# Seven-product up-projection in pairs of chunks: chunks 4 to 19 as eight interleaved pairs, 256-column weight blocks, low parts added by DMA

## The chip, the core and the metric

The kernel runs on one core of a Trainium2 chip. The metric is the device time of one execution in microseconds; the kernel before took 1119.47 us (median of three runs, 1118.79 to 1120.16). Engines are named as in the profile: PE is TensorE (matmuls), DVE is VectorE, ACT is ScalarE, POOL is GpSimd, SP is SyncE. SP issues the plain loads; POOL issues the DMAs that add to their target and some stores.

## The reference

Two decoder layers over a residual stream of 512 tokens by 1024 features: layer 0 with dilated window attention, layer 1 with forgetting attention, each followed by the same feed-forward block. Only that block concerns us here:

```python
def conv_ffn(xn, w_up, cw, cb, w_down):          # xn (1, 512, 1024), w_up (1024, 2 * 2816)
    a = xn @ w_up
    ap = jnp.pad(a, ((0, 0), (CONV_W - 1, 0), (0, 0)))
    a = sum(ap[:, j:j + T] * cw[j] for j in range(CONV_W)) + cb
    gate, val = jnp.split(a, 2, axis=-1)
    return (jax.nn.gelu(gate, approximate=True) * val) @ w_down
```

All data are 32-bit floats. The block's output goes through a root-mean-square norm with a gain (`norm_gains[l, 3]`) and is added to the residual.

## The kernel before

**Precision.** TensorE takes 32-bit operands in a reduced format. Each operand is therefore split into a high part (a copy to that format, made by ScalarE) and a low part (the operand less its high part). A product is three matmuls per 128 rows of the contraction: high by high, high by low, low by high (`mm3`, lines 283 to 285). A weight's low part is made in one of two ways: VectorE subtracts (`sub_low`, `Weights.low`), or ScalarE writes the negative of the raw weight, scaled copy with -1, in the reduced format, and a DMA issued by GpSimd adds the raw weight onto it (`add_low` at line 680, `Weights.low_added` at line 98).

**Chunks.** The up-projection runs over 22 chunks (`NF`). Chunk c has 128 gate columns and the 128 value columns with the same index, so two PSUM banks of 128 by 512 (features by tokens). After a chunk's products come its taps: ScalarE's Identity with the last tap and the bias (line 620), two VectorE operations that add the other two taps (621, 623), for the gate half and for the value half; then ScalarE's Gelu of the gate half (641) and VectorE's product of the halves (638), stored to `hD` in DRAM by a GpSimd DMA (636).

**Two ways to multiply.** A plain chunk (`up`) takes two weights of eight 128-row blocks, 48 matmuls over 512 tokens. A chunk of the tuple `SEVEN` is a 2 by 2 block product (gate and value by the two halves of the contraction; the two halves of the tokens) done with seven products in place of eight: 84 matmuls over 256 tokens. It needs sums of weight blocks, S1 to S4, on VectorE; sums of the activations, XA and XB, made once per layer (`sums_in`); and additions between partial results, done by VectorE in PSUM (lines 963 to 1007). Before, eleven chunks of each layer go by seven products, mostly two of them followed by a plain one; `weights_a` and `weights_b` prepare a chunk's weights one or two chunks ahead, and the generator `steps` places their parts between the products.

**Order and buffers.** All is under a manual schedule: each engine executes its instructions in the order of the program text, and waits where an operand is not ready. Pools give out buffers in the same order. `t8` (pool p8) has sixteen buffers of 8 KB per partition, for split weights and activations; in the up-projection eight of these hold the activations and their sums. `t4` (pool p4) has ten of 4 KB: raw weights, sums of weights (`wsum`), the taps' result `bb`, gains, and others outside this stage. `t2` has eight of 2 KB. PSUM has eight banks. A buffer can be given to a new tile after its tile's last use in program order; the new tile's first writer then waits until that use has really ended, a DMA's reading included.

**Weights.** `Weights` walks the list `pieces` in order. `load(n)` has SyncE issue loads up to piece n, `take(k)` hands out the next k raw pieces after loading `ahead_dma` further ones, `high_added()` splits a piece in the way with the DMA, and `get()` returns the next split piece.

**The end of the stage.** While the last chunks run, `pair_load`, `pair_sums`, `pair_highs` and `pair_lows` prepare the first steps of the down-projection (`down`), whose results go to the norm object `nxt`; its gain was loaded before `ffn` began.

Of the kernel before, what the change touches and what calls it, by code (L numbers as in the profile page):

```python
# [16 lines left out]
T = 512  # L17
# [10 lines left out]
SEVEN = 4, 5, 7, 8, 10, 11, 13, 14, 16, 17, 19  # L28

ADDED = (6, 9, 12, 15, 18), (18, 20)  # L30
# [87 lines left out]
def trunk_kernel(ctx, tc, x, norm_gains, w_qkv_a, w_o_a, w_q_b, w_o_b, kv_norm, w_kvf, b_f,  # L118
# [35 lines left out]
    def add(f):  # L154
        pieces.append(f)
# [22 lines left out]

    dT = [tc.dram_tile([ND, 128, 2048], F32, name=f"dT{l}") for l in range(2)]

    def add_ffn(l):
        for c in range(NF):
            add_cols(w_up[l], c * 128)
            add_cols(w_up[l], DFF + c * 128)

        for j in range(ND):
            add(lambda raw, j=j: [(raw[:, 0:512], w_down[l][j * 256:j * 256 + 128, 0:512]),
                                  (raw[:, 512:1024], dT[l][j, :, 0:512])])
            add(lambda raw, j=j: [(raw, dT[l][j, :, 512:1536])])
        add_rows(w_down[l], range(1, NF, 2))  # L190
# [420 lines left out]
    def ffn(l, bd, cp, nxt, ahead):  # L611
# [4 lines left out]
        def taps(c, banks, between=None):  # L616
            bb = t4([128, 2, T], name="bb")
            for s, ch in ((0, c), (1, NF + c)):
                ps = banks[s]
                act.activation(bb[:, s, :], ps, AF.Identity, bias=cp[:, 3, ch:ch + 1], scale=cp[:, 2, ch:ch + 1])  # L620
                dve.scalar_tensor_tensor(bb[:, s, 1:], ps[:, :T - 1], cp[:, 1, ch:ch + 1], bb[:, s, 1:],  # L621
                                         ALU.mult, ALU.add)
                dve.scalar_tensor_tensor(bb[:, s, 2:], ps[:, :T - 2], cp[:, 0, ch:ch + 1], bb[:, s, 2:],  # L623
                                         ALU.mult, ALU.add)
                if s == 0 and between is not None:
                    between()
            return bb

        gated = []

        def product():

            if gated:
                c, bb = gated.pop()
                if c - 1 in hc:
                    pool.dma_start(hD[c - 1], hc.pop(c - 1))
                hc[c] = t2([128, T], name="hc")
                dve.tensor_tensor(hc[c], bb[:, 0, :], bb[:, 1, :], ALU.mult)

        def glu(c, bb):  # L640
            act.activation(bb[:, 0, :], bb[:, 0, :], AF.Gelu_apprx_tanh)
            gated.append((c, bb))

        def post(c, banks, between=None):
            product()
            glu(c, taps(c, banks, between))
# [23 lines left out]
        halves, rest, late = {}, {}, []  # L670

        def split_pair(pair, src, n=1024):
            act.copy(pair[:, 0, :n], src)
            yield
            dve.tensor_tensor(pair[:, 1, :n], src, pair[:, 0, :n].bitcast(F32), ALU.subtract)

        def add_low(w, raw):

            act.activation(w[:, 1], raw, AF.Copy, scale=-1.0)
            pool.dma_start(w[:, 1], raw, accum_op=ALU.add)  # L680

        def sub_low(w, raw, n=1024):
            dve.tensor_tensor(w[:, 1, :n], raw, w[:, 0, :n].bitcast(F32), ALU.subtract)

        def weights_a(c):


            if c >= NF:
                return
            if c not in SEVEN:  # L690
                for i in range(2):
                    if c in ADDED[i]:
                        W.high_added()
                    else:
                        W.high()
                        W.low()
                    yield
                return
            r0, r1 = W.take(2)
            w = [t8([128, 2, 1024], F32R, name="w") for _ in range(2)]  # L700
            sa, sb = (t4([128, 1024], name="wsum") for _ in range(2))
            a11, a12, a21, a22 = r0[:, 0:512], r0[:, 512:1024], r1[:, 0:512], r1[:, 512:1024]
            act.copy(w[0][:, 0], r0)
            if c - 1 not in SEVEN:
                add_low(w[0], r0)
            dve.tensor_tensor(sa[:, 0:512], a11, a21, ALU.subtract)
            dve.tensor_tensor(sb[:, 0:512], a21, a22, ALU.add)
            yield
            dve.tensor_tensor(sa[:, 512:1024], sb[:, 0:512], a11, ALU.subtract)
            if c - 1 not in SEVEN:  # L710
                act.copy(w[1][:, 0], sa)
                add_low(w[1], sa)
            v = [t.rearrange("p s (q k c) -> p s q k c", q=2, k=4) for t in w]
            halves[c] = dict(A11=v[0][:, :, 0], A12=v[0][:, :, 1], S3=v[1][:, :, 0], S2=v[1][:, :, 1])
            rest[c] = w, r0, a12, a22, sa, sb

        def weights_b(c):

            if c not in rest:
                return  # L720
            (w0, w1), r0, a12, a22, sa, sb = rest.pop(c)
            if c - 1 in SEVEN:
                act.copy(w1[:, 0], sa)
                sub_low(w0, r0)
            w = [t8([128, 2, 1024], F32R, name="w") for _ in range(2)]
            dve.tensor_tensor(sb[:, 512:1024], a12, sa[:, 512:1024], ALU.subtract)
            act.copy(w[1][:, 0, 0:512], a22)
            if c - 1 in SEVEN:
                sub_low(w1, sa)
            yield  # L730
            act.copy(w[0][:, 0], sb)
            if c - 1 in SEVEN:
                late.append(lambda: sub_low(w[0], sb))
            else:
                add_low(w[0], sb)
            sub_low(w[1], a22, 512)
            v = [t.rearrange("p s (q k c) -> p s q k c", q=2, k=4) for t in w]
            halves[c].update(S1=v[0][:, :, 0], S4=v[0][:, :, 1], A22=v[1][:, :, 0])
            yield

# [186 lines left out]
        post(0, first[0:2])  # L930
        next(extra)
        post(1, first[2:4])
        W.ahead = 1
        W.split(base + 7)
        W.high_added()
        steps = iter(())
        begun = None
        before = None
        for c in range(2, NF):
            if c == NF - 4:  # L940
                pair_load(0)
            steps = chain(steps, weights_b(c + 1), weights_a(c + 2))
            if c + 2 == SEVEN[0]:
                steps = chain(steps, weights_b(c + 2))
            if c in SEVEN:
                w = halves.pop(c)
                W.n_get += 2
                x11, x21, x22 = [(xT[0][i], xT[1][i], s) for i, s in ((0, LO), (1, LO), (1, HI))]
                if begun:
                    banks, s1, s17 = begun  # L950
                else:
                    banks = [bank([128, T], name="up") for _ in range(2)]
                    s1, s17 = (t2([128, 256], name="csum") for _ in range(2))
                s12 = t2([128, 256], name="csum")
                o1, o2, o3, o4 = banks[0][:, LO], banks[0][:, HI], banks[1][:, LO], banks[1][:, HI]

                def prod(o, a, x, start=False, w=w):
                    half_mm(o, w[a], x[0:2], x[2], start)

                def begin():  # L960
                    act.copy(s1, o1)
                    prod(o3, "S3", (*XA, HI), True)
                    dve.tensor_tensor(s17, o3, s1, ALU.add)
                    prod(o2, "S2", (*XB, HI))

                def join():
                    dve.tensor_tensor(s12, o2, s1, ALU.add)

                if begun:
                    prod(o2, "S2", (*XB, HI))  # L970
                    product()
                    join()
                    bb = taps(*before)
                else:
                    prod(o1, "A11", x11, True)
                    product()
                    bb = taps(*before, begin)
                    join()
                prod(o3, "A22", (*XB, LO))
                prod(o1, "A12", x21)  # L980
                prod(o2, "S1", (*XA, LO))
                next(steps, None)
                glu(before[0], bb)
                next(steps, None)
                if c + 1 in SEVEN:
                    next(steps, None)
                dve.tensor_tensor(o4, o2, s17, ALU.add)
                if c + 1 in SEVEN:
# [10 lines left out]
                if c + 1 not in SEVEN:  # L999
                    next(steps, None)  # L1000
# [7 lines left out]
            else:  # L1008
                banks = [bank([128, T], name="up") for _ in range(1 if begun else 2)]
                if begun:  # L1010
                    w, first = begun
                    banks = [first, *banks]
# [802 lines left out]
```

## Time and profile before

| What | Value |
|---|---|
| median of three runs | 1119.47 us (1118.79 to 1120.16) |
| span of the profiled execution, first to last instruction | 1116.5 us |
| TensorE busy | 1100.3 us, 99% of the span |
| VectorE busy | 894.2 us, 80% |
| ScalarE busy | 680.4 us, 61% |
| GpSimd busy | 214.7 us, 19% |
| granted TensorE clock, mean | 0.998 |
| chain that ended last | PE 85%, DMA 6%, DVE 4%, issue 3% |

The profiled execution is shown by its span alone; its own whole time is not listed beside the runs, and the median of the runs lies 3.0 us above the span. A row of a timeline gives the start and the duration in us, the engine, the line of the kernel, the operation, output and inputs by the program's names, and in brackets the idle time before it and what ended it. Durations on one engine overlap, since an instruction's beginning runs beside the end of the one before: what an instruction costs its engine is the distance from start to start. The up-projection of layer 0 lies at about 208 to 417 us of the span, that of layer 1 at about 794 to 1005.

### The profile page before, as it was taken

The numbers are of one execution on the slowest core, as the hardware profiler recorded it, in microseconds if no ns is written. First come the engines' busy times: TensorE is split into PE (matmuls) and PEld (weight loads), VectorE is DVE, ScalarE is ACT, GpSimd is POOL, SyncE is SP. The second block draws the span as 40 slices with busy tenths as digits, with TensorE's granted clock in tenths as the row PEclk, the third lists the DMA queues.
The fourth block names the chain that finished last, engine by engine and source line by source line (L and its number), as shares of the span: only waits on it lengthen the run. The fifth ranks groups of instructions, "written<-read, shape, count | busy, mean of one in ns | idle before, by whom it ended". The sixth has DMA issues, their size and how long they took to land.

```text
span 1116.5 us, 18086 instructions
## 1 busy us (share of the span) xinstructions
PE 1100.3 (99%) x6545; PEld 958.5 (86%) x6545; DVE 894.2 (80%) x1509; ACT 680.4 (61%) x1128; POOL 214.7 (19%) x315
## 2 busy tenths in 40 slices
PE   9899999999999999999999999999999999999997
PEld 6788889999999988888878888889999999978886
DVE  5797778887788679997698687868887788679894
ACT  6454466656666747576462588756656666747572
POOL 2723000411111211000000545500411111211000
PEclk9999999999999999999999999999999999999999
DMA  5699964368878979894447666594468878979862
GB/s 193 234 371 408 348 190 122 82 179 204 199 186 188 249 254 320 297 321 113 132 151 256 216 161 168 186 283 120 84 180 203 202 183 188 244 242 321 314 245 75
DMA packets 186209, 240.46 MB, mean 215 GB/s; under 512 B 12608, under 2 KB 132408, under 8 KB 186120
## 3 DMA queue, kind: packets, MB, share of 16 engines
q1 hardware_dynamic: 171016, 186.61, 51.4%
q0 software_dynamic: 15104, 52.70, 20.7%
q8 instruction: 51, 0.84, 0.3%
q14 instruction: 38, 0.31, 0.1%
HBM read 166.08 MB, written 39.63 MB: 184 GB/s over the span
## 4 chain that ended last, share of the span: by engine, by line
PE 85%; DMA 6%; DVE 4%; issue 3%; ACT 1%; POOL 1%; DVEq 0%; SPq 0%; POOLq 0%; ACTq 0%
PE up L285 12%; PE up L283 12%; PE up L284 12%; PE acc L283 8%; PE acc L285 8%; PE acc L284 8%; DMA w<-wsum 2%; PE qk_ps L283 2%; PE qk_ps L284 2%; PE qk_ps L285 2%; PE o_ps L1692 2%; PE s_ps L1644 1%; PE first L285 1%; PE first L283 1%; PE first L284 1%
## 5 line engine op out<-in xcount | busy, mean ns | idle before, releaser
L283 PE MATMUL acc<-w 128*128 128x512 f32 (+1 forms) x311 | 120.6, 388 | 0.3 <-DVE mix L332 0.3
L285 PE MATMUL acc<-w 128*128 128x512 f32 (+1 forms) x311 | 120.4, 387 | 0.0
L284 PE MATMUL acc<-w 128*128 128x512 f32 (+1 forms) x267 | 103.2, 387 | 0.0
L285 PE MATMUL up<-xsh,w 128*128 128x256 f32 x352 | 99.8, 284 | 1.9 <-DMA w<-wsum 1.9
L283 PE MATMUL up<-xsh,w 128*128 128x256 f32 x352 | 99.6, 283 | 0.0
L284 PE MATMUL up<-xsl,w 128*128 128x256 f32 x352 | 99.6, 283 | 0.0
L78 DVE TENSOR_TENSOR w<-wraw,w 128x1024 fp32r<-128x1024 f32 x62 | 82.2, 1346 | 21.6 <-ACT w L60 21.0
L620 ACT ACTIVATE bb<-up,conv 128x512 f32<-128x512 f32 x80 | 59.6, 775 | 60.8 <-DVE up L1007 50.0
L60 ACT CAST w<-wraw 128x1024 fp32r<-128x1024 f32 x82 | 84.3, 1048 | 19.8 <-DMA dsums<-in_w_down_dram 6.9
L284 PE MATMUL up<-xcl,w 128*128 128x512 f32 (+1 forms) x276 | 93.5, 339 | 0.0
L284 PE MATMUL up<-xbl,w 128*128 128x512 f32 (+1 forms) x276 | 93.5, 339 | 0.0
L283 PE MATMUL up<-xch,w 128*128 128x512 f32 (+1 forms) x276 | 93.5, 339 | 0.0
L283 PE MATMUL up<-xbh,w 128*128 128x512 f32 (+1 forms) x276 | 93.5, 339 | 0.0
L285 PE MATMUL up<-xbh,w 128*128 128x512 f32 (+1 forms) x276 | 93.4, 338 | 0.0
L285 PE MATMUL up<-xch,w 128*128 128x512 f32 (+1 forms) x276 | 93.4, 338 | 0.0
L285 PEld LDWEIGHTS up<-xsh,w 128*128 128x128 f32 x352 | 67.6, 192 | 2.3 <-DMA w<-wsum 2.3
L283 PEld LDWEIGHTS acc<-w 128*128 128x128 f32 x311 | 58.4, 188 | 12.5 <-DVE mix L332 0.7
L285 PEld LDWEIGHTS acc<-w 128*128 128x128 f32 x311 | 58.4, 188 | 11.9
L283 PEld LDWEIGHTS up<-xsh,w 128*128 128x128 f32 x352 | 67.6, 192 | 0.0
L284 PEld LDWEIGHTS up<-xsl,w 128*128 128x128 f32 x352 | 67.6, 192 | 0.0
L621 DVE SCALAR_TENSOR_TENSOR bb<-up,conv,bb 128x511 f32<-128x511 f32 x80 | 59.5, 744 | 7.3 <-ACT bb L620 7.3
L623 DVE SCALAR_TENSOR_TENSOR bb<-up,conv,bb 128x510 f32<-128x510 f32 x80 | 59.9, 749 | 2.8
(312 smaller groups left out, 3190.9 us busy)
## 6 DMA issues: line engine op xcount, KB each, us to landing
wraw<-in_w_up_dram SPq DMA_DIRECT2D x88, 512.0 KB, 5.3
w<-wraw POOLq DMA_DIRECT2D x32, 512.0 KB, 6.3
dT<-dsums SPq DMA_DIRECT2D x28, 512.0 KB, 6.7
w<-wsum POOLq DMA_DIRECT2D x24, 512.0 KB, 5.6
dsums<-in_w_down_dram SPq DMA_DIRECT2D x22, 512.0 KB, 7.6
dsums<-in_w_down_dram SPq DMA_DIRECT2D x44, 256.0 KB, 7.0
hD<-hc POOLq DMA_DIRECT2D x44, 256.0 KB, 7.1
dact<-hD SPq DMA_DIRECT2D x44, 256.0 KB, 5.3
```

Of the source, the lines that this page charges most:

```text
L60: self.nc.scalar.copy(pair[:, 0], raw)
L78: self.nc.vector.tensor_tensor(pair[:, 1], raw, pair[:, 0].bitcast(F32), ALU.subtract)
L283: pe.matmul(o, ah, bh, start=first, stop=False, skip_group_check=shared)
L284: pe.matmul(o, ah, bl, start=False, stop=False, skip_group_check=shared)
L285: pe.matmul(o, al, bh, start=False, stop=last, skip_group_check=shared)
L620: act.activation(bb[:, s, :], ps, AF.Identity, bias=cp[:, 3, ch:ch + 1], scale=cp[:, 2, ch:ch + 1])
L621: dve.scalar_tensor_tensor(bb[:, s, 1:], ps[:, :T - 1], cp[:, 1, ch:ch + 1], bb[:, s, 1:], ALU.mult, ALU.add)
L623: dve.scalar_tensor_tensor(bb[:, s, 2:], ps[:, :T - 2], cp[:, 0, ch:ch + 1], bb[:, s, 2:], ALU.mult, ALU.add)
L1644: pe.matmul(s[hh][:, :nn], qT[j][:, m, hh, i * 128:(i + 1) * 128], k, start=m == 0, stop=m == 1)
L1692: pe.matmul(o[64 * hh:64 * hh + 64, i * 128:(i + 1) * 128], Vt[hd // 8][:, k, (hd % 8) * 64:(hd % 8) * 64 + 64], pT[j, i, hh][:, k, :], st ...
```

## The change

Chunks 4 to 19 of each layer now all go by seven products, two neighbouring chunks together as a `Pair`. Chunks 0 to 3, 20 and 21 stay plain. The weights of a pair are four blocks of 512 rows by 256 columns: A11 (gate, first half of the contraction), A21 (value, first half), A22 (value, second half), A12 (gate, second half). Sums and splits are made on whole blocks of 128 by 1024 elements per tile, and each of the seven products is done for both chunks in turn, 24 matmuls of 256 tokens. The products accumulate in PSUM: intermediate results that are needed twice are copied out by ScalarE (`keep`), and VectorE adds them back (`sum_1`, `sum_3`, `sum_4`). The low parts of A11, A12, A22 and S1 are added by GpSimd's DMA onto ScalarE's negatives; those of S2, S3 and S4 are subtracted by VectorE. The taps of the previous pair's two chunks, a and b, are placed between the products. The gain of the block's norm is loaded at the end of the loop and no longer before `ffn`; `ahead_dma` is 3 during the loop. Line numbers of the page are those of the kernel before.

```diff
-SEVEN = 4, 5, 7, 8, 10, 11, 13, 14, 16, 17, 19
-
-ADDED = (6, 9, 12, 15, 18), (18, 20)
+PAIRS = tuple(range(4, 20, 2))
...
+    def add_block(w, q, c):
+        add(lambda raw, q=q, c=c: [(raw.rearrange("p (k c) -> p k c", k=4), cols(w, 4 * q, 4, c, 256))])
...
         for c in range(NF):
-            add_cols(w_up[l], c * 128)
-            add_cols(w_up[l], DFF + c * 128)
+            if c in PAIRS:
+                for q, f in ((0, 0), (0, DFF), (1, DFF), (1, 0)):
+                    add_block(w_up[l], q, f + c * 128)
+            elif c - 1 not in PAIRS:
+                add_cols(w_up[l], c * 128)
+                add_cols(w_up[l], DFF + c * 128)
...
+            def tap(self, s):
+                if s == 0:
+                    self.bb = t4([128, 2, T], name="bb")
+                tap(self.bb, self.c, s, self.banks[s])
...
+            def s3(self):
+                self.add("S3", "A11", "A21", ALU.subtract, self.f["A21"])
...
+            def high(self, key, added=False):
+                self.t[key] = w = t8([128, 2, 1024], F32R, name="w")
+                act.copy(w[:, 0], self.f[key])
+                if added:
+                    act.activation(w[:, 1], self.f[key], AF.Copy, scale=-1.0)
+                    pool.dma_start(w[:, 1], self.f[key], accum_op=ALU.add)
+
+            def low(self, key):
+                w = self.t[key]
+                dve.tensor_tensor(w[:, 1], self.f[key], w[:, 0].bitcast(F32), ALU.subtract)
+
+            def prod(self, key, outs, x, s, start=False):
+                w = self.t.pop(key).rearrange("p s (k c) -> p s k c", k=4)
+                for i, o in enumerate(outs):
+                    half_mm(o, w[:, :, :, i * 128:i * 128 + 128], x, s, start)
...
+            def keep(self, banks, s):
+                t = t2([128, 2, 256], name="csum")
+                for i, o in enumerate(banks):
+                    act.copy(t[:, i], o[:, s])
+                return t
...
+            def p_7(self):
+                self.V = self.new_banks()
+                self.prod("S3", self.at(self.V, LO), XA, HI, True)
...
+            def sum_4(self):
+                for i, (g, v) in enumerate(zip(self.G, self.V)):
+                    dve.tensor_tensor(v[:, HI], g[:, HI], self.k7[:, i], ALU.add)
+                del self.k7
...
+        for i, p in enumerate(pairs):
+            W.n_get += 4
+            n, n2 = (pairs[i + k] if i + k < len(pairs) else None for k in (1, 2))
+            a, b = m[0], m[-1]
+            p.p_7()
+            if prev:
+                prev.sum_1()
+            a.tap(0)
+            p.high("A12", True)
+            p.keep_7()
+            p.p_6()
+            a.tap(1)
+            if n:
+                n.take("A21", "A22")
+                n.s1()
+            else:
+                W.high_added()
+            p.high("S4")
+            p.keep_2()
+            p.p_4()
+            a.gelu()
+            if prev:
+                b.tap(0)
+            a.product()
+            p.low("S4")
+            p.p_5()
+            p.sum_3()
+            if n:
+                n.s3()
+            if prev:
+                b.tap(1)
+            if n:
+                n.high("A22", True)
+                n.p_1()
+            else:
+                W.high_added()
+                begun = W.get(), bank([128, T], name="up")
+                up(*begun, range(4))
+            p.sum_4()
+            if n:
+                n.high("S3")
+            if prev:
+                b.gelu()
+            if n:
+                n.high("S1", True)
+            p.p_2()
+            if n:
+                n.s2()
+            if prev:
+                b.product()
+            if n:
+                n.take("A12")
+                n.s4()
+                n.keep_1()
+            else:
+                W.high_added()
                 pair_load(0)
...
+            p.p_3()
+            if n:
+                n.high("S2")
+            if n2:
+                n2.take("A11")
+                n2.high("A11", True)
+            if n:
+                n.low("S3")
+                n.low("S2")
+            prev, m = p, p.chunks()
+
+        W.ahead_dma = 2
+        W.high_added()
+        nxt.mix.gain = load_gain(gain, f"gain{l}3")
+        pair_sums(0)
...
-    bd2 = SharedBoundary(load_gain(norm_gains[0, 3], "gain03"), gcol, "xk")
-    ffn(0, bd, cp[0], bd2, 4)
+    bd2 = SharedBoundary(None, gcol, "xk")
+    ffn(0, bd, cp[0], bd2, norm_gains[0, 3], 4)
...
-    ffn(1, bd, cp, Final(load_gain(norm_gains[1, 3], "gain13")), 0)
+    ffn(1, bd, cp, Final(None), norm_gains[1, 3], 0)
```

More of the change, by code (lines that the diff above doesn't have):

```diff
@@ L717, in weights_b, with X @@
[L717 to L739, printed above, removed]
+        def X(i):
+            return xT[0][i], xT[1][i]
```

301 lines of the change are left out of this document (139 added, 162 removed).

## The prediction

> **What bounds the kernel now.** I read the page's busy times first, then TensorE's waits.
>
> ```profile
> PE 1100.3 (99%) x6545; PEld 958.5 (86%) x6545; DVE 894.2 (80%) x1509; ACT 680.4 (61%) x1128; POOL 214.7 (19%) x315
> ```
>
> ```profile
> PE up L285 <- DMA w<-wsum: 1.9, 2, 1.7
> ```
>
> TensorE (PE) is the bound and waits for almost nothing; in the up-projection its only wait is 1.9 us for a low part that a DMA adds. So a change can win only by giving TensorE less to do, and can lose by making one of the other engines, now at 61 to 80%, too late. What TensorE's work costs is read from the starts of matmuls, since their durations overlap. The next rows are TensorE's timeline (start, duration, then the operation): chunks 2 and 3 run from the first row to the second, the first four products of chunk 4 from the second to the third.
>
> ```profile
> 207.69 0.40 PE L283 MATMUL up<-xbh,w 128*128 128x512 f32 x1
> ...
> 229.47 0.28 PE L283 MATMUL up<-xbh,w 128*128 128x256 f32 x1
> ...
> 235.23 0.28 PE L283 MATMUL up<-xbh,w 128*128 128x256 f32 x1
> ```
>
> 96 matmuls of 512 columns take 21.78 us, 0.227 each; 48 of 256 columns take 5.76 us, 0.120 each. A plain chunk (48 of 512) costs 10.89 us, a seven-product chunk (84 of 256) 10.08 us, one product of a pair (24 of 256) 2.88 us, a pair 20.16 us.
>
> How near is the stage of before to that? The view of the tile up gives its first and last starts in both layers:
>
> ```profile
> L285 PE MATMUL up<-xbh,w x276: 283/389/389, 208.2 to 417.0; 128*128 128x512 f32 x72, 128*128 128x256 f32 x66
> ...
> L285 PE MATMUL up<-xch,w x276: 283/389/389, 794.2 to 1004.6; 128*128 128x512 f32 x72, 128*128 128x256 f32 x66
> ```
>
> Eleven seven-product and nine plain chunks make 110.9 + 98.0 = 208.9 us. The first of these starts is the third matmul (0.45 in), the last is the final one (0.23 before the end): 208.2 us without a stall. The rows say 208.8 and 210.4, so 0.6 and 2.2 us, 2.8 together, are lost.
>
> **What the change takes from TensorE.** Per layer 16 chunks go by seven products and four stay plain: 161.3 + 43.6 = 204.9 us, 4.0 less; 8.1 us less in two layers. If all stalls went too, the most it can win is 10.9 us, 1%. The rest is whether VectorE, ScalarE and the transfers hold the new pace of 20.16 us per pair.
>
> **VectorE and ScalarE per pair.** Both overlap an instruction's tail with the next, so I cost by start-to-start times. Timeline of VectorE, then of ScalarE, then of GpSimd:
>
> ```profile
> 255.30 0.74 DVE L621 SCALAR_TENSOR_TENSOR bb<-up,conv,bb 128x511 f32<-128x511 f32 x1
> 256.07 0.75 DVE L623 SCALAR_TENSOR_TENSOR bb<-up,conv,bb 128x510 f32<-128x510 f32 x1
> 256.74 0.68 DVE L726 TENSOR_TENSOR wsum<-wraw,wsum 128x512 f32<-128x512 f32 x1
> 257.34 0.68 DVE L683 TENSOR_TENSOR w<-wraw,w 128x512 fp32r<-128x512 f32 x1
> ...
> 261.12 0.75 DVE L621 SCALAR_TENSOR_TENSOR bb<-up,conv,bb 128x511 f32<-128x511 f32 x1 [0.49 <-ACT bb L620]
> ...
> 263.68 0.42 DVE L963 TENSOR_TENSOR csum<-up,csum 128x256 f32<-128x256 f32 x1 [1.03 <-PE up L285]
> 264.02 0.74 DVE L621 SCALAR_TENSOR_TENSOR bb<-up,conv,bb 128x511 f32<-128x511 f32 x1
> ...
> 265.80 1.21 DVE L683 TENSOR_TENSOR w<-wraw,w 128x1024 fp32r<-128x1024 f32 x1
> 266.93 0.68 DVE L726 TENSOR_TENSOR wsum<-wraw,wsum 128x512 f32<-128x512 f32 x1
> ```
>
> ```profile
> 246.03 0.64 ACT L641 ACTIVATE bb<-bb 128x512 f32<-128x512 f32 x1 [0.55 <-DVE bb L623]
> 246.56 1.03 ACT L703 CAST w<-wraw 128x1024 fp32r<-128x1024 f32 x1
> ...
> 258.42 1.05 ACT L679 ACTIVATE w<-wsum 128x1024 fp32r<-128x1024 f32 x1
> 259.38 1.04 ACT L703 CAST w<-wraw 128x1024 fp32r<-128x1024 f32 x1
> 260.32 0.77 ACT L620 ACTIVATE bb<-up,conv 128x512 f32<-128x512 f32 x1
> ...
> 262.19 0.38 ACT L961 COPY csum<-up 128x256 f32<-128x256 f32 x1 [1.10 <-PE up L285]
> 262.46 0.79 ACT L620 ACTIVATE bb<-up,conv 128x512 f32<-128x512 f32 x1
> 263.13 1.04 ACT L723 CAST w<-wsum 128x1024 fp32r<-128x1024 f32 x1
> ```
>
> ```profile
> 259.76 0.85 POOL L680 DMA_DIRECT2D w<-wsum  x1 [5.30 <-ACT w L679]
> ```
>
> VectorE: two taps on one half 0.77 + 0.67 = 1.44; 512 columns 0.60; 1024 columns 1.13; 256 columns 0.34. A pair needs four tap pairs (5.8), the four sums S1 to S4 at 1024 columns (4.5; no such sum is in the trace of before, which takes 512 at a time, so between 1.13 of the equal-sized low part and 2 x 0.60; I take 1.13), three low parts (3.4), two gate products (1.2) and six sums of 256 (2.0): 16.9 us of 20.16. ScalarE: seven high parts and four negatives at 0.96 (10.6), four Identities at 0.67 (2.7), two Gelus at 0.53 (1.1), six PSUM copies at 0.27 (1.6): 16.0 us. GpSimd issues four added low parts and two stores of 0.85: 5.1. None exceeds 20.16, but all run in order and hand to each other, so waits count.
>
> **The wait that the new order adds.** The pool of 4 KB buffers has ten. I count who is alive in the loop when `b.tap(0)` asks for the buffer bb of the second chunk: bb of the first (its product comes after), S4 of this pair (its low part comes after), A11, A21, A22 and A12 of the next pair, A11 and A21 of the pair after (loaded by `n.take("A21", "A22")`, which with `ahead_dma` 3 reaches two pieces into it), and S1 of the next: nine. Before them this pair's own A12 had its last use, as the addend of its low part. So bb is the tenth and must take the last buffer free. The other candidates ended with the pair before (a product, a low part S3, a low part S2 or S1's added part); A12 ends last of all, with a DMA that starts only in this turn. I take it that bb gets A12's buffer: `b.tap(0)` on ScalarE then waits until A12's added part has landed. Queued behind it on ScalarE are `b.tap(1)` and the high parts A22, S3, S1 and S2 of the next pair; on VectorE the taps of b, and behind them everything else of the pair. Before, such buffers go to raw loads, where the wait costs nothing, as SyncE's waits show; for the landings I read the views of lines 680 and 98, the two places that add low parts by DMA:
>
> ```profile
> SPq L50 <- DMA w<-wraw: 74.5, 10, 23.5
> ```
>
> ```profile
> DMA to landing us min/median/max: 5.0/6.1/10.0
> ```
>
> ```profile
> DMA to landing us min/median/max: 4.6/7.3/8.4
> ```
>
> I take 6.1, the median of the 36 of line 680, issued like these between sums, and keep 5.0 and 8.4 for the range.
>
> Now the ring, from one `a.tap(0)` to the next. ScalarE: Identity 0.67, A12 high 0.96, its negative to its end 1.05. To GpSimd 0.29 (259.76 less 258.42 + 1.05). Landing 6.1. ScalarE: Identity of b to its end 0.79. VectorE, in program order: taps of b 1.44, product of a 0.60, low S4 1.13, sum_3 0.68, S3 1.13, taps of b's second half 1.44, sum_4 0.68, S2 1.13, product of b 0.60, S4 1.13, low S3 1.13, low S2 1.13, sum_1 to its end 0.77; then ScalarE may begin the next `a.tap(0)`. That is 3.47 + 0.29 + 6.1 + 12.99 = 22.85, and four hand-overs (0.03 to VectorE by the row at 261.12; up to 0.1 elsewhere) make 23.0 us. TensorE's seven products need 20.16, so each full turn costs 2.8: `p_7` waits 1.1 for the low part S3 and `p_3` waits 1.7 for sum_4.
>
> Per layer: the first turn has no second chunk and leaves VectorE ahead, which hides nearly all in the second turn (0.2); turns three to seven cost 2.8 each, 14.0; the last finds other buffers free but begins 1.1 late, loses 0.5, and then waits for the first low part of chunk 20, which ScalarE has finished 7.5 us into the turn, so that it lands at 13.9, where TensorE is there at 11.9: 2.0. Sum 17.8 us per layer. What hides the rest: the next pair's A11 ends on ScalarE about 11 us before `p_1` needs it, A22 and S1 13 or more, so at 6.4 they cost nothing; at the 10.3 of the slowest landing they still fit.
>
> One-off edits: 2 x 512 KB of gains load at the end of the loop instead of before it, far ahead of their use; PSUM stays at eight banks, and the next pair's two come from the first chunk's taps, which are over by then. In front of the loop TensorE has four plain products of 5.45 us while VectorE prepares the first pair; I cost that at nothing (0 to 3 us if a raw block comes late).
>
> The sum: 1116.5 us of span and the 3.0 by which the runs' median lies above it make 1119.5. Minus 8.1, minus 2.8 of old stalls, plus 2 x 17.8 = 35.6: **1144 us**.
>
> The Trainium skill, "DMA: Bandwidth & Descriptors", section "Anatomy of one DMA — SWDGE (gpsimd) path", gives a transfer of this queue 2.0 us plus its bytes at 436 GB/s, an estimate of 3.2 us for 512 KB; the ring would then be 20.1 us and the wait free, about 1112 us. The rows of before have no landing under 4.6, so I go by them. "Perfetto Trace Analysis", section "Identifying Performance Opportunities", reads the same gap repeated on the busiest engine as a sign that buffers ran out; that is the picture I expect.
>
> **The rivals.** (1) *The tenth buffer goes elsewhere*: a raw load takes A12's buffer and bb an older one. Then the loop's ring has no DMA; VectorE's 16.9 plus its two holes for ScalarE (0.9 before the first taps, 1.7 before the second) stay under 20.16, and TensorE loses only the wait for chunk 20, 1.5 per layer: 1119.5 - 10.9 + 3.0 = 1112 us, faster. For it: raw loads take such buffers in before. Against: by the count there is one buffer left and one taker. It decides if the landing stops mattering, from a ring of 20.16 down, a landing of 3.3. (2) *VectorE is the bound without that wait*: if whole durations count instead of start-to-start times, 16.9 becomes about 18.4, with the holes and a gap per instruction 22.3: 2.1 x 7 x 2 = 30 more, 1139 us. Against: the rows at 265.80 and 266.93. (3) *The DMA engines fill up*:
>
> ```profile
> 250.00:281.00 31.00, 31.00 (x217) 29.09 (x216) 25.04 (x40) 19.52 (x25) 5.12 (x7) 1.00 0.83 195
> ...
> 374.00:405.00 31.00, 30.82 (x182) 27.27 (x181) 20.27 (x34) 17.80 (x23) 5.12 (x8) 1.00 0.98 267
> ```
>
> In windows of 31 us (last columns: clock, DMA share, GB/s) six raw and four added blocks fill 0.83; four and four in 20.16 us would be up to 1.02, at 23.0 still 0.90. Later landings then: at 8.4 the ring is 25.3, loss 33.5 per layer, 1176 us. 0.98 was held with 0.18 us lost, so I give the far end little. (4) *Landings under every row*, as the page's fit has them: at 4.6 the ring is 21.5 and the loss 7.5 per layer, 1123 us; at 3.3 or less the result is that of (1).
>
> **How the numbers follow.** The forecast has 0.64 (its own range, landings of 5.0 to 7.3: 1129 to 1161), rival 1 0.19, rival 2 0.06, rival 3 0.06, rival 4 0.05, of which 0.02 reaches (1)'s time. Faster needs (1) or that: 0.21; within 0.2% (2.2 us, about what this kernel's measurement tells from no change) 0.03; slower 0.76. The range must reach to (1) to leave out no more than 2 in 10: 1110 to 1163.
>
> **What would show it.** Right: ScalarE's waits have the Identity of the taps waiting for the DMA of a `w`, some 6 times per layer, 3 us each; in the loop TensorE waits 1.1 and 1.7 us per pair for VectorE, starts of `p_7` 23 us apart. Wrong: starts 20.2 us apart and no such wait (rival 1); ScalarE without DMA waits, VectorE over 95% busy (rival 2); landings over 8 us and a DMA share near 1 (rival 3). The saving itself is wrong if 256-column matmuls in the loop start over 0.120 apart.

## The result, and the profile after

The changed kernel takes 1181.72 us (median of four runs, 1179.72 to 1182.70) against 1119.56 of the kernel before: a ratio of 1.0558, 95% interval 1.0540 to 1.0576. It is slower, as forecast, but by 62 us where the forecast had 25. The profiled execution has a span of 1180.9 us.

Busy times of the page of the changed kernel (share of the span in brackets):

```profile
PE 1120.7 (95%) x6905; PEld 993.6 (84%) x6905; DVE 894.9 (76%) x1453; ACT 731.9 (62%) x1228; POOL 233.7 (20%) x337
```

TensorE is busy for 20 us more than before although it has less to do, and it now has gaps. Where the stage lies, by the view of the tile up (first and last start of the third matmul of each triple; line 290 is line 285 of before):

```profile
L290 PE MATMUL up<-xbh,w x256: 278/283/795, 208.3 to 451.1; 128*128 128x256 f32 x96, 128*128 128x512 f32 x32
...
L290 PE MATMUL up<-xch,w x256: 278/283/797, 829.0 to 1069.0; 128*128 128x256 f32 x96, 128*128 128x512 f32 x32
```

The two stages take 242.8 and 240.0 us where their matmuls need 204.2 from the same first to the same last start: 38.6 and 35.8 us lost, 74 in all, of which the 10.9 that the change can save have to be taken off: 63.5, about the difference measured. The forecast had 17.8 lost per layer. TensorE's and ScalarE's waits (total us, times, longest):

```profile
PE up L288 <- DVE up L770: 39.0, 12, 5.1
PE up L290 <- DMA w<-wraw: 6.9, 2, 4.7
...
ACT bb L623 <- DMA w<-wraw: 38.8, 12, 5.1
```

The last row is the forecast wait: the Identity of `b.tap(0)` waits for a DMA of a low part, six times per layer, 3.2 us each. TensorE stands where it was not forecast: before `p_2`, for `sum_4` (line 770). One turn of it, in GpSimd's timeline (the added parts of A11, A12, A11, A12), ScalarE's (`b.tap(0)`), VectorE's (`sum_4`) and TensorE's (end of `p_5`, then `p_2`):

```profile
300.45 0.85 POOL L708 DMA_DIRECT2D w<-wraw  x1 [1.97 <-ACT w L707]
305.20 0.85 POOL L708 DMA_DIRECT2D w<-wraw  x1 [3.90 <-ACT csum L728]
...
327.09 0.85 POOL L708 DMA_DIRECT2D w<-wraw  x1 [1.96 <-ACT w L707]
332.12 0.85 POOL L708 DMA_DIRECT2D w<-wraw  x1 [4.18 <-ACT csum L728]
```

```profile
314.04 1.44 ACT L623 ACTIVATE bb<-up,conv 128x512 f32<-128x512 f32 x2 [4.23 <-DMA w<-wraw]
...
339.40 1.45 ACT L623 ACTIVATE bb<-up,conv 128x512 f32<-128x512 f32 x2 [2.67 <-DMA w<-wraw]
```

```profile
321.27 0.75 DVE L770 TENSOR_TENSOR up<-up,csum 128x256 f32<-128x256 f32 x2
```

```profile
317.23 0.28 PE L290 MATMUL up<-xbh,w 128*128 128x256 f32 x1
321.75 0.58 PE L288 MATMUL up<-xbh,w 128*128 128x256 f32 x1 [4.25 <-DVE up L770]
322.13 0.42 PE L289 MATMUL up<-xbl,w 128*128 128x256 f32 x1
```

A12's added part holds `b.tap(0)` from 305.20 to 314.04, 8.8 us, and in the next turn from 332.12 to 339.40, 7.3 us; the forecast had 6.1. Just ahead of it, 4.8 and 5.0 us earlier, GpSimd has issued the added part of the next pair's A11. From one A11 to the next are 26.6 us here, not 23.0. This is a long turn: over both layers the starts of `b.tap(0)` lie 25.6 us apart on average (ten intervals), and the twelve added parts of A12 land 6.6 to 8.9 us after their issue, 7.7 on average.

The second wait is the one at chunk 20, once per layer (TensorE's timeline, 512 columns):

```profile
417.44 0.40 PE L289 MATMUL up<-xbl,w 128*128 128x512 f32 x1
422.50 0.80 PE L290 MATMUL up<-xbh,w 128*128 128x512 f32 x1 [4.66 <-DMA w<-wraw]
423.09 0.63 PE L288 MATMUL up<-xbh,w 128*128 128x512 f32 x1
423.51 0.63 PE L289 MATMUL up<-xbl,w 128*128 128x512 f32 x1
```

This one, in layer 0, lasts about 4.8 us beyond a normal start, that of layer 1 (2.63 us from start to start) 2.4, where 2.0 was forecast; behind it the matmuls start 0.43 us apart and not 0.227. The same is seen behind the gap before `p_2`: the first start of 256 columns comes 0.38 after its predecessor and not 0.120. In the stretch of the pairs (window in us; sum, busy TensorE, its weight loads, VectorE, ScalarE, GpSimd; granted clock, DMA share, GB/s) the granted clock is 0.91:

```profile
250.00:410.00 160.00, 139.10 (x1068) 137.88 (x1067) 105.23 (x143) 100.32 (x144) 28.17 (x37) 0.91 0.77 182
```

The DMA share of 0.77 is a mean of two states. While the added parts of A11 and A12 are under way, with raw loads beside them, the engines are full; behind them they stand nearly still:

```profile
300.00:312.00 12.00, 12.00 (x102) 12.00 (x102) 5.41 (x8) 6.25 (x11) 2.27 (x3) 1.00 1.03 243
312.00:319.00 7.00, 5.51 (x46) 5.30 (x45) 4.12 (x7) 3.34 (x4) 0.85 (x1) 1.00 0.06 18
```

### The profile page after: what moved, and what is told of

Read it like the earlier page. It is cut to its first block, busy times and chain, and to the rows that moved or that the text cites. A ratio compares the mean times of both kernels' runs of the same rounds, so it can differ in the third digit from the quotient of the medians.

```text
span 1180.9 us, 19004 instructions
## 1 busy us (share of the span) xinstructions
PE 1120.7 (95%) x6905; PEld 993.6 (84%) x6905; DVE 894.9 (76%) x1453; ACT 731.9 (62%) x1228; POOL 233.7 (20%) x337
## 4 chain that ended last, share of the span: by engine, by line
PE 53%; issue 15%; DMA 12%; DVE 12%; ACT 5%; POOL 2%; POOLq 0%; DVEq 0%; SPq 0%; ACTq 0%
DMA w<-wraw 9%; PE acc L288 8%; PE acc L290 7%; PE acc L289 7%; PE up L288 4%; PE up L290 4%; PE up L289 4%; DVE bb L624 2%; PE qk_ps L289 1%; PE qk_ps L288 1%; PE qk_ps L290 1%; ACT w L705 1%; DVE bb L625 1%; DVE wraw L689 1%; DVE w L712 1%
## 5 line engine op out<-in xcount | busy, mean ns | idle before, releaser
L288 PE MATMUL up<-xsh,w 128*128 128x256 f32 x512 | 144.9, 283 | 0.0
L289 PE MATMUL up<-xsl,w 128*128 128x256 f32 x512 | 144.9, 283 | 0.0
L290 PE MATMUL up<-xsh,w 128*128 128x256 f32 x512 | 144.9, 283 | 0.0
L288 PE MATMUL up<-xbh,w 128*128 128x256 f32 (+1 forms) x256 | 85.1, 332 | 20.9 <-DVE up L770 20.9
L288 PE MATMUL up<-xch,w 128*128 128x256 f32 (+1 forms) x256 | 86.4, 337 | 18.1 <-DVE up L770 18.1
L288 PEld LDWEIGHTS up<-xsh,w 128*128 128x128 f32 x512 | 98.3, 192 | 0.0
L290 PEld LDWEIGHTS up<-xsh,w 128*128 128x128 f32 x512 | 98.3, 192 | 0.0
L708 POOL DMA_DIRECT2D w<-wraw x48 | 41.0, 853 | 242.1 <-ACT w L707 152.9
L290 PE MATMUL up<-xbh,w 128*128 128x256 f32 (+1 forms) x256 | 84.4, 330 | 4.7 <-DMA w<-wraw 4.7
L705 ACT CAST w<-wraw 128x1024 fp32r<-128x1024 f32 x64 | 66.8, 1044 | 34.6 <-DVE wraw L689 34.6
L290 PE MATMUL up<-xch,w 128*128 128x256 f32 (+1 forms) x256 | 85.6, 334 | 2.2 <-DMA w<-wraw 2.2
L289 PE MATMUL up<-xcl,w 128*128 128x256 f32 (+1 forms) x256 | 85.2, 333 | 0.0
L289 PE MATMUL up<-xbl,w 128*128 128x256 f32 (+1 forms) x256 | 84.3, 329 | 0.0
L58 ACT CAST w<-wraw 128x1024 fp32r<-128x1024 f32 x62 | 63.7, 1051 | 19.3 <-PE v_ps L289 6.9
L288 PEld LDWEIGHTS up<-xbh,w 128*128 128x128 f32 x256 | 54.0, 211 | 24.7 <-DVE up L770 22.1
```

The lines of the kernel that those rows point to most:

```text
L58: self.nc.scalar.copy(pair[:, 0], raw)
L288: pe.matmul(o, ah, bh, start=first, stop=False, skip_group_check=shared)
L289: pe.matmul(o, ah, bl, start=False, stop=False, skip_group_check=shared)
L290: pe.matmul(o, al, bh, start=False, stop=last, skip_group_check=shared)
L705: act.copy(w[:, 0], self.f[key])
L708: pool.dma_start(w[:, 1], self.f[key], accum_op=ALU.add)
```

## The experiments

All edits are to the changed kernel. The ratios are to the kernel before on the same chip.

**One load fewer ahead.** Theory A: the buffer wait of `b.tap(0)` makes the loss. Rivals: B, VectorE's and ScalarE's own work doesn't fit; C, the DMA engines are full.

```diff
+        W.ahead_dma = 2
         for i, p in enumerate(pairs):
```

> One load fewer is kept ahead in the loop over the pairs, so one 4 KB buffer fewer is alive and b's bb takes a buffer that VectorE or an earlier DMA freed long before; every operation stays. Theory A (the buffer wait of b.tap(0), 12 x 3.2 us on ScalarE, closed into a ring by p_2's wait for sum_4): that wait goes, the ring falls to about 21 us a pair, p_2 still waits about 0.8 us a pair for sum_4, about 7 to 8 us lost per layer with the wait at chunk 20: 1108.6 + 2 x 7.1 to 8.3, 1123 to 1125 us. Theory B (VectorE's and ScalarE's own work and hand-overs do not fit in 20.16 us; the buffer wait only takes up slack): 1165 or more. Theory C (the DMA engines are too full, the loads arrive late): with less loaded ahead not faster, 1175 to 1190.

Measured: 1117.1 us, ratio 1.0001 (0.9980 to 1.0023). TensorE's waits and the same window as above:

```profile
PE up L290 <- DMA w<-wraw: 5.2, 2, 2.9
```

```profile
250.00:410.00 160.00, 157.73 (x1241) 153.99 (x1241) 124.93 (x176) 119.95 (x170) 34.91 (x47) 0.99 0.95 238
```

Of the 74 us lost in the two stages 62 are gone (their first and last starts lie 209.3 and 211.1 us apart), and TensorE has no wait left inside the pairs. B falls, since no operation was taken away, and so does C: the DMA engines are now at 0.95 where they were at 0.77, and nothing in the pairs waits for them. Theory A's number was 6 to 8 us too high, of which 2.7 are the kernel before being faster on this chip (1116.84); the wait of 0.8 us a pair at `p_2` that it kept isn't there.

**The buffer freed earlier instead.** Loads stay as far ahead; A12's raw block is given free by VectorE.

```diff
-            p.high("A12", True)
+            p.high("A12")
+            p.low("A12")
```

> VectorE makes A12's low part instead of a negative on ScalarE and a DMA that adds; loads as far ahead as in the changed kernel, so bb still takes A12's buffer, but that buffer is free 2 us after a.tap(0) instead of 8 to 9. VectorE has 1.13 us more per pair, 18.0 of 20.16. Theory A: as without the buffer wait but with a ring 1.1 us longer, about 22.1 a pair: 13 to 16 us lost per layer, 1135 to 1141 us. Theory B (VectorE's work sets the pace): more work on VectorE, 1185 or more. Theory C (full DMA engines): one added block fewer of four, a quarter of the loss gone, about 1165.

Measured: 1123.18 us, ratio 1.0053 (1.0034 to 1.0072). TensorE's first wait:

```profile
PE up L290 <- DMA w<-wraw: 8.6, 2, 4.3
```

No wait is left inside the pairs, although VectorE has 1.13 us more per pair. So it isn't the smaller number of loads that helps, but that bb's buffer comes free. Again the number was too high (1135): VectorE, in this order, holds 20.16 us with 18.0 of work.

**`sum_4` earlier, with the wait kept.** Is the detour of the ring over `p_2` the part that the forecast lacked?

```diff
             if n:
                 n.s3()
+            p.sum_4()
             if prev:
                 b.tap(1)
...
-            p.sum_4()
```

> sum_4 moves in VectorE's order ahead of the second taps of b; the buffer wait stays. Theory A with the PSUM dependence of p_2 on sum_4: the ring loses 1.44 us of taps between the landing and p_2; by the prediction's start-to-start costs 22 to 30 us lost per layer instead of 36 to 38: 1155 to 1168 us. Rival (p_2 does not need sum_4, TensorE follows the ScalarE and VectorE ring of the prediction): the order of two VectorE operations leaves that ring's length as it is, 1178 to 1184 us.

Measured: 1180.07 us, ratio 1.0575 (1.0544 to 1.0606), not to be told from the changed kernel. The expectation of theory A missed, that of the rival is met, though not for the reason it gives: `p_2` waits for `sum_4` in this run too, 12 times, 37.9 us in all. GpSimd's and ScalarE's timelines, same operations as above:

```profile
300.94 0.85 POOL L708 DMA_DIRECT2D w<-wraw  x1 [1.96 <-ACT w L707]
304.68 0.85 POOL L708 DMA_DIRECT2D w<-wraw  x1 [2.89 <-ACT csum L728]
...
326.60 0.85 POOL L708 DMA_DIRECT2D w<-wraw  x1 [1.96 <-ACT w L707]
330.07 0.85 POOL L708 DMA_DIRECT2D w<-wraw  x1 [2.63 <-ACT csum L728]
```

```profile
313.54 1.45 ACT L623 ACTIVATE bb<-up,conv 128x512 f32<-128x512 f32 x2 [4.25 <-DMA w<-wraw]
...
338.91 1.45 ACT L623 ACTIVATE bb<-up,conv 128x512 f32<-128x512 f32 x2 [4.90 <-DMA w<-wraw]
```

A12's part is issued earlier behind A11's (3.7 and 3.5 us instead of 4.8 and 5.0) and takes longer for it, 8.9 and 8.8 us: in both kernels `b.tap(0)` comes 12.3 to 12.6 us after A11's issue (13.6 in the first turn shown of the changed kernel). And from `b.tap(0)` to the next A11's issue are 13.05 us in both (314.04 to 327.09; 313.54 to 326.60). 13.05 + 12.3 to 13.6 are the 25.4 to 26.6 us of a turn. By these rows the ring closes over A11's added part, and an A12 issued sooner only waits longer behind it. The next three runs test that.

**A11's added part off GpSimd's queue.** VectorE makes it in the hole in which it waits for `b.tap(0)`.

```diff
                 n.take("A21", "A22")
                 n.s1()
+                if prev:
+                    n.low("A11")
...
-                n2.high("A11", True)
+                n2.high("A11")
```

> From the second turn on VectorE makes A11's low part, in the hole of some 5 us in which it waits for b.tap(0), instead of a negative and an adding DMA that GpSimd issues 3.4 to 5 us ahead of A12's. The buffer wait stays. Theory L (A12's added part lands in 7.2 to 8.9 us and not in 6.1 because A11's is still under way): its landings fall to about 5.6, what the first one of each pair takes; the ring falls with them to 22.5 us over VectorE and 23.3 over p_2, sum_1 and the taps, 17 to 20 us lost per layer instead of 36 to 38: 1143 to 1150 us. Rival (landings are long because the DMA engines are full, or TensorE's slow matmuls after each gap keep the ring long): landings stay at 7 to 8 and the time within 8 us of the changed kernel's.

Measured: 1152.51 us, ratio 1.0319 (1.0294 to 1.0344). GpSimd's timeline (A12 alone now) and ScalarE's, then TensorE's waits:

```profile
300.44 0.85 POOL L708 DMA_DIRECT2D w<-wraw  x1 [6.21 <-ACT csum L728]
...
322.90 0.85 POOL L708 DMA_DIRECT2D w<-wraw  x1 [5.49 <-ACT csum L728]
```

```profile
306.30 1.45 ACT L623 ACTIVATE bb<-up,conv 128x512 f32<-128x512 f32 x2 [1.26 <-DMA w<-wraw]
328.89 1.45 ACT L623 ACTIVATE bb<-up,conv 128x512 f32<-128x512 f32 x2 [2.16 <-DMA w<-wraw]
```

```profile
PE up L288 <- DVE up L770: 20.5, 12, 3.6
PE up L290 <- DMA w<-wraw: 8.8, 2, 4.6
```

A12 now takes 5.9 and 6.0 us, the turn shown 22.5, and the loss at `p_2` is halved. Over both layers the starts of `b.tap(0)` lie 23.2 us apart on average. By the ratios, taking that one transfer out of GpSimd's queue is worth 27 us, 2.4% of the time; but some of VectorE's and ScalarE's work has moved with it. The time is 2.5 us above what was expected.

**The same with `sum_4` earlier** (both diffs together).

> The same, and sum_4 ahead of b's second taps. With the ring over p_2 cut by 1.44 us, what is left is the ring of the prediction over VectorE, 22.2 to 22.5 us with landings of 5.6: 13 to 17 us lost per layer, 1135 to 1143 us. If only the ring over VectorE decides, as the first run with sum_4 moved suggests, it is within 3 us of the kernel without that move.

Measured: 1152.13 us, ratio 1.0320 (1.0294 to 1.0347): no difference to the run without the move. `sum_4` is where TensorE stands; it isn't what sets the pace.

**Only the order of the two transfers.** The operations of the changed kernel, but GpSimd issues A11's added part right behind A12's.

```diff
-            def high(self, key, added=False):
+            def high(self, key, added=False, now=True):
...
-                    pool.dma_start(w[:, 1], self.f[key], accum_op=ALU.add)
+                    if now:
+                        self.add_low(key)
+
+            def add_low(self, key):
+                pool.dma_start(self.t[key][:, 1], self.f[key], accum_op=ALU.add)
...
             p.high("A12", True)
+            if n and prev:
+                n.add_low("A11")
...
-                n2.high("A11", True)
+                n2.high("A11", True, False)
```

> Same operations and the same loads ahead; only GpSimd issues the adding DMA of A11 (of the next pair) right behind A12's instead of 3.4 to 5 us ahead of it, from the second turn on. In the changed kernel the two have both landed 12.2 to 12.5 us after the first was issued, about twice the 5.6 to 6.1 of one alone. Theory Q (added parts go mostly one behind the other, in order of issue): A12's now land in 5.6 to 7, A11's in 10 to 12; b.tap(0) waits 2 us less, its ring falls to some 23 us, but p_1 now waits for A11: issued about 5 us into a turn, landed at 16, needed at 11.5, 4 to 5 us a turn: 1165 to 1185 us. Theory H (they share evenly, so that either ends when both are done): A12's land in 10 to 12, the ring becomes 16.75 + 11, 28 us a pair, and p_1 waits too: 1205 to 1230 us.

Measured: 1152.70 us, ratio 1.0307 (1.0284 to 1.0329). GpSimd's timeline (both parts in one row now), ScalarE's and TensorE's second wait:

```profile
299.19 1.74 POOL L712 DMA_DIRECT2D w<-wraw  x2 [5.43 <-ACT csum L732]
...
323.23 1.73 POOL L712 DMA_DIRECT2D w<-wraw  x2 [5.42 <-ACT csum L732]
```

```profile
306.71 1.45 ACT L623 ACTIVATE bb<-up,conv 128x512 f32<-128x512 f32 x2 [3.62 <-DMA w<-wraw]
329.32 1.45 ACT L623 ACTIVATE bb<-up,conv 128x512 f32<-128x512 f32 x2 [2.18 <-DMA w<-wraw]
```

```profile
PE up L290 <- DMA w<-wraw: 11.1, 6, 4.2
```

A12 takes 7.5 and 6.1 us, a turn 23.4 us on average, and the ratio is that of the two runs before, some 28 us less than with A11 in front. So the place of A11's transfer alone does it, and not the work of ScalarE and VectorE that those runs had moved as well. Both theories on how the two share the queue missed the time: neither does A11 take 10 to 12 us behind A12 (6.8 to 9.7 in the loops; of the six waits in the last row two are chunk 20's, so `p_1` waits for it four times), nor do the two share evenly. Issued together, both have landed 7 to 10 us after the first issue; issued 3.5 to 5.5 us apart, 11 to 14. Counted from the second issue the two cases are alike (6.8 to 9.7 and 6.6 to 8.9): its head start gains A11's transfer nothing. In the changed kernel S1's added part, issued 3.4 us ahead of A11's in each full turn of layer 0, is then still under way, and the DMA engines are full (1.03 above); which of these holds A11's back, or whether it is the queue's order, wasn't tried.

**`sum_4` behind `p_2`, without the buffer wait.** Does `p_2` stand before `sum_4` because the two use one PSUM bank?

```diff
+        W.ahead_dma = 2
...
-            p.sum_4()
...
             p.p_2()
+            p.sum_4()
```

> One load fewer ahead, and sum_4 behind p_2 in the order of the program. If p_2 and sum_4 exclude each other because they use one PSUM bank (p_2 its low half, sum_4 reads its high half), sum_4 now starts only after p_2, p_3 waits for it about 1 us in each of eight turns, and VectorE's order behind it is late: 16 to 24 us over the kernel with one load fewer, 1132 to 1142. If the halves are independent, p_2 no longer waits for anything and sum_4 runs as before: 1113 to 1118 us.

Measured: 1145.29 us, ratio 1.0257 (1.0237 to 1.0278). VectorE's longest wait, TensorE's, and the two halves of `sum_4` in one turn:

```profile
DVE up L770 <- PE up L290: 58.1, 32, 7.7
...
PE up L290 <- DVE w L712: 18.7, 14, 1.4
```

```profile
290.76 0.43 DVE L770 TENSOR_TENSOR up<-up,csum 128x256 f32<-128x256 f32 x1 [1.33 <-PE up L290]
292.20 0.43 DVE L770 TENSOR_TENSOR up<-up,csum 128x256 f32<-128x256 f32 x1 [1.01 <-PE up L290]
```

The time is 3 us above the expectation of the first case. Now `sum_4` waits for `p_2`, 1.44 us from half to half, the time of the 12 matmuls that write one bank. It reads the tokens' second half of that bank and `p_2` writes the first. So in this program the two exclude each other though they touch different halves, and whichever stands first in the text goes first. One tile fills one bank, so this run doesn't tell whether the waiting goes by tile or by bank. The price is not at `p_3`, as expected, but at `p_7`, which then waits 1.3 us in 14 turns (18.7 / 14) for the low part S3.

**Both edits, and then chunk 20.** One load fewer and `sum_4` earlier; then, in a further kernel, also the first low part of chunk 20 by VectorE:

```diff
             else:
-                W.high_added()
+                W.high()
+                W.low()
             p.high("S4")
```

> Both edits: one load fewer ahead, and sum_4 ahead of b's second taps. Theory A: no wait inside the pairs is left, only about 2.4 us per layer for the first added low part of chunk 20: 1108.6 + 2 x 2.4 to 3.6, 1113 to 1116 us, faster than before. Theories B and C: no nearer to before than the single edits, 1150 or more.

> One load fewer ahead and sum_4 earlier, and the first low part of chunk 20 by VectorE instead of a DMA. The 2.4 and 1.8 us that TensorE waited there should go, with the few slow matmuls behind them: 1113.6 less 4 to 5, 1108 to 1110 us. If VectorE is itself late there (its taps and low S4 run in the same 12 us), the wait stays at 1 us or more: 1111 to 1114.

Measured: 1113.60 us, ratio 0.9966 (0.9953 to 0.9979), for the two; 1108.99 us, ratio 0.9929 (0.9911 to 0.9948), for the three; both times lie in what was expected. Chunk 20 in the kernel with one load fewer, and in the kernel with both edits:

```profile
387.13 0.40 PE L289 MATMUL up<-xbl,w 128*128 128x512 f32 x1
389.80 0.80 PE L290 MATMUL up<-xbh,w 128*128 128x512 f32 x1 [2.27 <-DMA w<-wraw]
390.39 0.63 PE L288 MATMUL up<-xbh,w 128*128 128x512 f32 x1
390.82 0.63 PE L289 MATMUL up<-xbl,w 128*128 128x512 f32 x1
```

```profile
384.23 0.40 PE L289 MATMUL up<-xbl,w 128*128 128x512 f32 x1
386.66 0.50 PE L290 MATMUL up<-xbh,w 128*128 128x512 f32 x1 [2.03 <-DMA w<-wraw]
387.00 0.40 PE L288 MATMUL up<-xbh,w 128*128 128x512 f32 x1
```

The stage and the window in the kernel with all three:

```profile
L290 PE MATMUL up<-xbh,w x256: 283/283/389, 208.4 to 412.6; 128*128 128x256 f32 x96, 128*128 128x512 f32 x32
...
L290 PE MATMUL up<-xch,w x256: 283/283/389, 790.4 to 994.6; 128*128 128x256 f32 x96, 128*128 128x512 f32 x32
```

```profile
250.00:410.00 160.00, 160.00 (x1261) 156.72 (x1260) 131.57 (x183) 122.47 (x173) 34.07 (x46) 1.00 0.96 243
```

Both stages take 204.2 us, which is the forecast's figure without any stall. By the ratios this version beats both kernels: by 0.7% the one before, by 6% the changed one.

## Why the prediction was right and wrong

**The saving: right in the stages.** 8.1 us less of matmuls and 2.8 of old stalls, 10.9 at most. The kernel without waits takes 204.2 us in both stages, 4.6 and 6.2 less than before, so 10.8. Its time of 1109.0 is near the 1108.6 that this gives in part by luck, since the kernel before took 1117.52 on that chip: by the ratio the whole kernel gains 7.9 us (5.8 to 10.0). Where the rest of the 10.8 goes is open.

**VectorE 16.9 and ScalarE 16.0 of 20.16: right.** The kernel without waits holds 20.16 a pair; its busy times of 131.57 and 122.47 in 160 us are 16.6 and 15.4 a pair. Even 18.0 on VectorE cost nothing inside the pairs. The rival of a VectorE that is too slow by itself falls.

**The tenth buffer: right.** Twelve waits of `b.tap(0)` for a DMA, 3.2 us each, as counted. Two different edits that free the buffer take the loss in the pairs away. The rival in which the buffer goes elsewhere had 1112; built on purpose, it gives 1117.1 (ratio 1.0001), and 1113.6 with `sum_4` moved.

**The landing of 6.1 us: the term that failed.** The step says "I take 6.1, the median of the 36 of line 680, issued like these between sums". A12's are not issued like these: A11's added part of the next pair goes out 3.5 to 5.5 us ahead on the same queue, and A12's takes 7.7 on average, up to 8.9. The text did look at A11's transfer, and wrote that it ends "about 11 us before `p_1` needs it" and so costs nothing. That holds for its own reader; what it does to the transfer behind it was not asked. With A11's out of the way A12's takes 5.8 on average, with A11's issued behind it 6.2, and the forecast's ring of 23.0 us is met: 23.2 and 23.4 on average in these two kernels, where the changed kernel has 25.6. By the forecast's own ring a landing of 7.7 instead of 6.1 makes 24.6; the missing 1.0 goes with the ring closing over A11's transfer (the rows of the run with `sum_4` earlier), which the forecast put at nothing. In ratios the changed kernel is at 1.056, these two at 1.031 to 1.032, the forecast was 1144 / 1119.5 = 1.022. So of the 38 us that were missing, some 27 are this term.

**The wait at chunk 20, 2.0 us per layer: mis-sized by the same cause and a second one.** It is 4.8 us in layer 0 and 2.4 in layer 1 here, and 4.4 in the average of the run without A11's transfer (8.8 over two), since this added part also lands late: 10.0 us after its issue in layer 0 of that run, where the forecast had 6.4. Behind it nine or ten matmuls of 512 columns start 0.43 apart in that run, another 2 us. In that run, at 1.032, this makes 2 x (4.4 + 2 - 2.0), about 9 us: nearly all of the 11 that were left.

**The slow starts: no term at all.** The sum had every wait cost its own length. In the stretch of the pairs the granted clock is 0.91, where before it was 1.00. At chunk 20 this is the 2 us just named; what it costs inside the pairs, where the ring sets the pace, the runs don't separate. When the clock falls stands in the last section.

**TensorE's waits of 1.1 at `p_7` and 1.7 at `p_3`: wrong place.** It waits at `p_2` for `sum_4`, 3.25 us twelve times (39.0 / 12), because `p_2` writes into the bank that `sum_4` reads; the forecast let only `p_3` wait, which writes the half that `sum_4` reads. The Trainium skill, "PSUM — Partial Sum Buffer", section "Summary: rules for kernel authors", says to let a read beside running matmuls go to another bank and to guard by bank; the late `sum_4` agrees, waiting 58.1 us for matmuls. The slip had no price of its own: as long as the buffer wait stands, moving `sum_4` changed nothing measurable, with A11's transfer in front or without it. Before that run I had taken it for the missing part.

**The rival of full DMA engines** had the time nearest to the result, 1176 us at landings of 8.4. Its price was about right. Its cause, engines full over the whole turn, didn't come: the mean share was 0.77, and at 0.95 and 0.96, without the buffer wait, nothing in the pairs was lost. But while A11's and A12's parts are under way the share is 1.03, so full engines may have a part in the 7.7. They don't make it alone: in the run without A11's transfer the share is 1.05 from 300 to 305, and A12's, issued at 300.44, lands in 5.8 us. The far end of the landings deserved more than the 0.06 that hung on this cause; so the range stopped at 1163.

**Landings under every row** didn't come: none of the 64 added parts of the pairs (line 708) lands faster than 4.5 us. The fit of the Trainium skill, "DMA: Bandwidth & Descriptors", section "Anatomy of one DMA — SWDGE (gpsimd) path", an estimate of 3.2 us for these bytes, is below every one of them. Here the measurement decides.

## What to carry to other kernels

When a new tile takes over a buffer, find out whose last use comes before it; if that is a DMA, its landing becomes part of the schedule, and one piece loaded less far ahead can be worth more than the work saved. Price such a landing from transfers with the same neighbours on their queue, and ask of every transfer what it delays behind it, not only whether its own reader can wait. Where an engine stands still isn't yet what sets the pace: follow the ring once around, and move the suspected operation before believing it.

## What was not expected of the hardware

A wait can cost TensorE more than its length, and when it comes decides as much as how long it is. At chunk 20, a gap of 2.43 us from start to start (384.23 to 386.66) was followed by one start 0.34 later and then the usual ones; a gap of 2.67 (387.13 to 389.80) by one of 0.59 and further ones of 0.43, nearly twice 0.227, and one of 5.06 the same. But before `p_2` in the changed kernel a gap of 2.67 us (266.95 to 269.62) was followed by starts 0.12 apart from the second on, and one of only 2.41 (913.61 to 916.02) by starts 0.21 apart from 917.4 on. The windows around these two (columns as above: after the sum comes TensorE's busy time, third from the end the granted clock):

```profile
265.48:268.89 3.41, 1.75 (x15) 1.55 (x13) 3.38 (x6) 1.08 (x2) 0.85 (x1) 1.00 0.60 117
...
914.01:917.42 3.41, 1.40 (x11) 1.40 (x12) 3.38 (x7) 3.20 (x4) 0.00 (x0) 1.00 1.00 192
917.42:920.84 3.42, 3.42 (x18) 3.42 (x17) 3.42 (x5) 3.42 (x6) 1.44 (x2) 0.50 0.85 256
```

In every trace of this case the granted clock changes only at times that lie whole multiples of 3.41 us apart. Between 200 and 460 and between 780 and 1075 us, where the up-projections lie, it fell to 0.50 behind each such stretch at full clock in which TensorE was idle for 57% or more (50 stretches; 59% in the second row), and behind none with 20 to 55% (54 stretches; 49% in the first row, and 1.00 in the stretch behind it). The busy time goes by the profile's modelled ends of matmuls, so the limit is only as exact as these. At chunk 20 of the kernel with one load fewer such a stretch ended at 389.82, just behind the start at 389.80.

The Trainium skill, "TensorE: Matmul & The Clock Gate", section "Part 1: The HAM clock gate (the "warmup" mystery)", has a clock that falls to half after an idle window of about 3.4 us, the windows running free of the kernel. The multiples of 3.41 us and the half rate agree; but a stretch need not be idle throughout here, 57% of it was enough, and the measurement decides.
